# Nine places of raw weights for seven and twelve units for fourteen; the residual leaves SBUF during cross-attention; a weight split moves ahead of a sum

## The chip, the core and the metric

The kernel runs on one core of one Trainium2 chip. The time is device microseconds of one execution; the median of several runs counts. A core has a matmul engine (TensorE, in the profile PE, its weight loads PEld), VectorE (DVE), ScalarE (ACT), GpSimd (POOL) and SyncE (SP). Each engine takes its instructions in a fixed order and waits on semaphores. SyncE issues most DMAs here, GpSimd some. SBUF is the on-chip memory that the engines work in, PSUM holds the matmuls' sums in eight banks.

## The reference

Two layers work on one residual stream `x` of 256 rows by 2048 columns in f32. Each layer has three sub-layers, each behind an RMS norm and added to `x`:

```
x = x + attention(rms_norm(x))          # layer 0: differential attention, layer 1: latent attention
x = x + cross_attention(rms_norm(x), mem_h)   # 256 memory rows, 4 heads of 128
x = x + square(relu(rms_norm(x) @ wup)) @ wdown     # 2048 -> 8192 -> 2048
```

A last RMS norm closes it. All weights are f32, some 410 MB in all.

## The kernel before, in words

**The products.** TensorE works on pairs of rounded parts: every f32 operand is split into a high half (a rounded copy) and a low half (the rest), and a product is three matmuls: high by high, high by low, low by high (`unit_part`, L238 to L249). The activations live split in SBUF in tiles called units (`unit`, 8 KB of each partition). The weights are loaded a block of 512 by 512 at a time (1 MB, 8 KB of each partition) into a raw tile; `halves_of` (L205) splits it in two pieces. For each piece ScalarE writes the high half (`whi`, L201) and VectorE the low half (`wlo`, L202). There are four buffers for each half, so at most four pieces are ahead of TensorE.

**The pools.** `wraw` has `RAWS` = 7 places for raw tiles, `units` has `UNITS` = 14 places for units. Both kinds of places have the same size. A load into a raw tile waits until the tile that had its place before has been read for the last time.

**What sets the order.** TensorE's order is written out by hand: the program keeps a clock of its own and puts small tasks (transposes, attention) between the products (`Task`, `pump`). The DMAs stay in the order in which the program issues them (`load`, L173). The orders of VectorE, ScalarE and GpSimd are chosen when the program is built: a scheduler estimates when each operand is there and takes, of what it thinks is ready, what stands earliest in the source. On the chip each engine then waits at whatever instruction stands next. `fill` (L215) keeps four weight blocks split ahead in the source, and fetches the next block's raw data once more ahead.

**The MLP's up projection.** Its 8192 columns come in eight blocks. Block 0 is done plainly. Blocks 1 to 7 use Strassen's scheme (`Seven`, L819): the 2 by 2 blocks of rows and columns of activations and weights are combined, so that seven products p1 to p7 do the work of eight. Each product has two steps (x = 0, 1), each of one raw tile. The combined activations (`Forms`) are made at the end of cross-attention on VectorE (L454, L471, L443). The combined weights are made in place: `add` (L843) is a VectorE sum of two raw tiles, 2048 elements wide. The tile t is loaded with the 12 block; for p5 the 11 block is added to it, for p6 the 22 block is added to it, for p2 the 21 block; behind p3's split GpSimd issues an accumulating DMA that adds the 12 block into the 22 tile for p7 (L835). So each block has six L843 sums: two for p5, two for p6, two for p2. The results of the products are combined on VectorE (L915, L919, L922). Steps of the down projection of earlier blocks are put between the products by a planner (`mlp_line`).

**The p2 job.** Its function first adds the 21 tile to t (L873), then splits the 21 tile. The sum reads the 21 tile and changes t, the split reads the 21 tile alone; p4 later uses t.

**The residual.** `x` lies in DRAM (`xd`, eight pieces of 128 by 512) for most of the time. Sub-layers that don't need its rows add to it with an accumulating DMA on GpSimd's queue (L504). `fetch_residual` (L506) allocates two units and loads the rows on GpSimd's queue, 8 DMAs of 256 KB; `store_residual` (L513) stores one piece. The last group of an attention (`project_group` with `nxt`, L1172) fetches it, adds its product in SBUF (`add_residual`, L500), and feeds the next norm (squares on ScalarE at L379, transposes on TensorE at L163). The two units then stay in use through cross-attention. `project_out` (L1162) adds cross-attention's product to the same tiles, feeds the forms of the MLP's norm, and stores the pieces. A norm's `row_norm` takes the power of -0.5 on GpSimd (L385), so this stands in GpSimd's order with the DMAs.

Of the kernel before, what the change touches and what calls it, by code (L numbers as in the profile page):

```python
# [21 lines left out]
CH = 512  # L22
EPS = 1e-6
WARM = 9
RAWS = 7
MLP_BLOCKS = 8
SEVEN = (1, 2, 3, 4, 5, 6, 7)
EVS = 7
UNITS = 14

T_EV, T_TURN, T_ROT, T_SM, T_SQ, T_ADD, T_NORM, T_SUM = 2.6, 2.6, 12.0, 6.5, 4.4, 2.2, 7.2, 3.0

# [16 lines left out]
def trunk(ctx, tc, x, xT, xT0, mem, memT, positions, gcols, gfinal, lam_vecs, consts, W, out):  # L49
    nc = tc.nc  # L50

    def pool(name, bufs, space=None):
        kw = {"space": space} if space else {}
        return ctx.enter_context(tc.tile_pool(name=name, bufs=bufs, **kw))

    keep = pool("keep", 1)
    wraw = pool("wraw", RAWS)
    whalf = pool("whalf", 4)
    units = pool("units", UNITS)
    work = pool("work", 2)  # L60
# [10 lines left out]
    def unit():  # L71
        return units.tile([P, 2, 4, S], F32R, tag="unit", name=nm("unit"))
# [92 lines left out]
    def f32(ap):  # L165
        return ap.bitcast(F32)
# [5 lines left out]
    def load(dst, src, queue=None):  # L172
        tc.keep_in_program_order((queue or nc.sync).dma_start(dst, src))  # L173
# [31 lines left out]
    def halves_of(raw, n=4 * CH, pieces=2):  # L205
        split = split_pieces(raw, n, pieces)
        for _ in range(pieces):
            split.next()
        return split.halves
# [41 lines left out]
    def matmul_chunk(acts, width=CH, turns=False, by_k=False):  # L251


        ps = [bank("mm") for _ in range(NT)]
        n = len(acts)

        def part(u, h, hi, lo, t):
            unit_part(ps[t][:, :width], acts[u], h, hi, lo, t, u == 0, u == n - 1)

        def ready_unit(u):  # L260
            need(acts[u].tasks)

        for u in range(n - 2 if turns else n):
            for h, (hi, lo) in enumerate(take()):
                ready_unit(u)
                if by_k and u == 0:
                    for k in range(2):
                        at = slice(k * width, (k + 1) * width)
                        for t in range(NT):
                            ah, al = acts[0].get(0, 2 * h + k, t), acts[0].get(1, 2 * h + k, t)  # L270
                            mm3(ps[t][:, :width], ah, al, hi[:, at], lo[:, at], h + k == 0, False)
                    continue
                for t in range(NT):
                    part(u, h, hi, lo, t)
        if turns:
            parts = [(u, h, *w) for u in (n - 2, n - 1) for h, w in enumerate(take())]
            for u in (n - 2, n - 1):
                ready_unit(u)
            for t in range(NT):
                for p in parts:  # L280
                    part(*p, t)
        return ps
# [214 lines left out]
    def add_residual(t, c, ps, later=False):  # L497
        if not later:
            xc = xs[t][:, c * CH : (c + 1) * CH]
            nc.vector.tensor_tensor(xc, xc, ps, ALU.add)  # L500
            return
        e = work.tile([P, CH], F32, tag="ev", name=nm("add"), bufs=EVS)
        nc.scalar.copy(e, ps)  # L503
        tc.keep_in_program_order(nc.gpsimd.dma_start(xd[t][c], e, accum_op=ALU.add))  # L504

    def fetch_residual():  # L506
        for t in range(NT):
            xs[t] = f32(unit()).rearrange("p a k t -> p (a k t)")
        for c in range(4):
            for t in range(NT):  # L510
                load(xs[t][:, c * CH : (c + 1) * CH], xd[t][c], nc.gpsimd)

    def store_residual(t, c):  # L513
        load(xd[t][c], xs[t][:, c * CH : (c + 1) * CH], nc.gpsimd)
# [304 lines left out]
    class Seven:  # L819
# [21 lines left out]
        def job(self, p, x):  # L841
            def add(o, q):
                nc.vector.tensor_tensor(o, o, q, ALU.add)  # L843

            loads = {"p5": (("t", x), (0, 1)), "p6": ((22, x), (1, 1)), "p2": ((21, x), (1, 0))}

            def fetch():
                key, (i, j) = loads[p]
                if key not in self.raw:
                    self.raw[key] = self.fetch(i, j, x)  # L850

            def run():
                r = self.raw
                if p in loads:
                    fetch()
                if p == "p1":
                    r[11, x] = o = self.fetch(0, 0, x)
                elif p == "p5":
                    o = r["t", x]
                    add(o, r.pop((11, x)))  # L860
                elif p == "p6":
                    o = r["t", x]
                    add(o, r[22, x])
                elif p == "p3":
                    o = r[22, x]
                    split = halves_of(o)
                    self.fetch(0, 1, x, o)
                    return split
                elif p == "p7":
                    o = r.pop((22, x))  # L870
                elif p == "p2":
                    o = r.pop((21, x))
                    add(r["t", x], o)  # L873
                else:
                    o = r.pop(("t", x))
                return halves_of(o)

            if p in loads:
                run.fetch = fetch
            return run  # L880
# [280 lines left out]

    def project_out(acts_o, gcol):  # L1162
        nxt = Forms(gcol)
        for c in range(4):
            ps = matmul_chunk(acts_o)
            for t in range(NT):
                add_residual(t, c, ps[t])
                nxt.feed(c, t, ps[t])
                store_residual(t, c)
        return nxt  # L1170

    def project_group(o, nxt=None, each=None):  # L1172
        if nxt:
            fetch_residual()
        for c in range(4):
            ps = matmul_chunk([o])
            if each:
                each(c)
            for t in range(NT):
                add_residual(t, c, ps[t], not nxt)  # L1180
                if nxt:
                    nxt.feed(c, t, ps[t])

    def attention(project, attend, mid, gcol):


        held = project(0)
        last = None
        m = []
        for gi in range(4):  # L1190
            o = Held(unit())
            attend(held, o)
            if last is not None:
                project_group(last, each=(lambda c: m.append(given_unit(memT, c, G_MEM))) if gi == 3 else None)
            if gi < 3:
                held = project(gi + 1)
            mid(gi)
            last = o
        mk = mem_keys(m)
        nxt = Stream(gcol)  # L1200
        project_group(last, nxt)
        return nxt, m, mk

    def cross(l, norm, m, mk):
        a = norm.done()
        rq = keep2(norm.rstd, SC_CA, "rq")
        q = Held(unit())
        ps = matmul_chunk(a)
        for t in range(NT):
            heads_T(ps[t], t, rq[t], q)  # L1210
        o = Held(unit())
        mv = []
        attend4(
            lambda h, first: whole(q, mk, h, S), q.tasks + mk.tasks,
            lambda: mv[0] if mv else None, o, False,
        )
        mv.append(mem_values(m))
        return project_out([o], G_MLP + 16 * l)
# [360 lines left out]
def build(a, w):  # L1579
    import concourse.bacc as bacc  # L1580

    nc = bacc.Bacc("TRN2", target_bir_lowering=False, num_devices=1, dynamic_dma_scratch_size=1024)
    arrays = {}

    def dram(name, v):
        arrays[f"in_{name}_dram"] = v
        return nc.dram_tensor(f"in_{name}_dram", v.shape, mybir.dt.from_np(v.dtype), kind="ExternalInput").ap()

    args = [dram(k, a[k]) for k in ("x", "xT", "xT0", "mem", "memT", "positions", "gcols", "gfinal", "lam_vecs", "consts")]
    weights = {k: dram(k, v) for k, v in w.items()}  # L1590
    o = nc.dram_tensor("out_0_dram", (S, D), F32, kind="ExternalOutput").ap()
    with tile.TileContext(nc, schedule_with_timeline_sim=True) as tc, tc.manual_schedule(engines={mybir.EngineType.PE}):
        trunk(tc, *args, weights, o)
    return nc, arrays
# [8 lines left out]
```

## Time and profile before

| what | value |
|---|---|
| median of 3 runs | 2225.3 us (2225.22 to 2227.26) |
| the profiled execution | 2232.52 us |
| its span, first to last instruction | 2230.8 us |
| mean granted clock of TensorE | 0.997 |
| HBM read, written | 459.24 MB, 37.75 MB |

How to read the profile: times count from the span's start. In a timeline a row is start, duration, engine, line, operation, output and inputs by the program's names, shapes, number of merged instructions, and in brackets the idle time before it with what ended it. In the waits a row is who waited for whom: total time, how often, the longest. In the busy times by stretch the columns are the length, then busy time (and number) of PE, PEld, DVE, ACT, POOL, then the granted clock of TensorE, the busy share of the DMA engines, and GB/s. The chain is the work that ended last, followed back. A row of DMA issues ends with the median time from issue to landing. Matmuls of 128x512 overlap: a row's duration is longer than its share of time.

Attention and cross-attention of layer 0 fill the first 500 us, its MLP the time to about 1180; layer 1 follows, with its MLP from about 1540 to the end.

### The profile page before, as it was taken

What the parts mean: (1) busy time and instruction counts of PE and PEld (TensorE: products, weight loads), DVE (VectorE), ACT (ScalarE), POOL (GpSimd) and SP (SyncE); (2) the same over time, 40 slices, a digit from 0 to 9 for tenths busy, and PEclk for the clock granted to TensorE, in tenths of its full rate; (3) what the DMA queues carried; (4) which work ended last, traced back from release to release, by engine and by line L of the source; (5) the groups of instructions that cost most, each with busy time, mean ns of one, the idle gap of its engine ahead of it and who ended that gap; (6) DMA issues with size and microseconds to landing.
All of it is one profiled execution on the core that took longest, in us unless ns stands there. A gap on an engine that the chain in (4) does not pass through costs nothing.

```text
span 2230.8 us, 28094 instructions
## 1 busy us (share of the span) xinstructions
PE 2209.2 (99%) x10559; PEld 1847.0 (83%) x10559; DVE 1673.8 (75%) x1801; ACT 1413.6 (63%) x1929; POOL 260.5 (12%) x390
## 2 busy tenths in 40 slices
PE   9999999999999999999999999999999999999998
PEld 7888888888888888887889988888888888888786
DVE  6665657789778788788665877668987887887864
ACT  6555646666766666666655766656766666666664
POOL 1212212000000000000100422201000000000011
PEclk9999999999999999999999999999999999999999
DMA  9457668446967876876955466935778678678691
GB/s 388 190 160 259 198 220 262 181 170 203 288 196 237 256 215 234 261 212 219 293 216 194 138 187 207 304 130 193 260 227 245 208 261 237 209 256 240 195 327 66
DMA packets 89785, 498.83 MB, mean 224 GB/s; under 512 B 10672, under 2 KB 11056, under 8 KB 37680
## 3 DMA queue, kind: packets, MB, share of 16 engines
q1 hardware_dynamic: 65232, 423.09, 51.6%
q0 software_dynamic: 24128, 73.41, 16.9%
q8 instruction: 83, 1.36, 0.2%
q10 hardware_dynamic: 288, 0.52, 0.1%
q14 instruction: 54, 0.44, 0.1%
HBM read 459.24 MB, written 37.75 MB: 223 GB/s over the span
## 4 chain that ended last, share of the span: by engine, by line
PE 81%; DVE 7%; DMA 5%; issue 4%; ACT 2%; POOL 1%; DVEq 0%; ACTq 0%; POOLq 0%
PE mm L159 59%; PE pr L159 17%; DMA raw<-in_mlp_wup_dram 5%; DVE wlo L202 4%; PE ax L159 3%; PE ax L163 2%; ACT whi L201 1%; PE mm L163 1%; DVE raw L843 1%; DVE unit L342 0%; DVE raw L471 0%; DVE unit L443 0%; POOL rs L385 0%; ACT p L1236 0%; ACT p L1237 0%
## 5 line engine op out<-in xcount | busy, mean ns | idle before, releaser
L202 DVE TENSOR_TENSOR wlo<-raw,whi 128x1024 fp32r<-128x1024 f32 (+2 forms) x962 | 1149.6, 1213 | 405.6 <-ACT whi L201 386.4
L201 ACT CAST whi<-raw 128x1024 fp32r<-128x1024 f32 (+2 forms) x962 | 998.4, 1041 | 642.3 <-PE mm L159 535.9
L159 PE MATMUL mm<-whi,unit 128*128 128x512 f32 (+3 forms) x4416 | 1394.4, 388 | 2.1 <-DVE unit L342 1.3
L159 PEld LDWEIGHTS mm<-whi,unit 128*128 128x128 f32 x4416 | 824.9, 188 | 164.4 <-DVE unit L342 2.2
L159 PE MATMUL mm<-wlo,unit 128*128 128x512 f32 (+3 forms) x2208 | 851.2, 386 | 0.8 <-DVE wlo L202 0.8
L159 PE MATMUL pr<-whi,unit 128*128 128x512 f32 x1568 | 508.4, 393 | 6.9 <-DVE p L919 6.9
L159 PEld LDWEIGHTS mm<-wlo,unit 128*128 128x128 f32 x2208 | 415.3, 188 | 79.0 <-DVE wlo L202 2.6
L159 PEld LDWEIGHTS pr<-whi,unit 128*128 128x128 f32 x1568 | 295.9, 189 | 70.7 <-issue 9.7
L159 PE MATMUL pr<-wlo,unit 128*128 128x512 f32 x784 | 307.7, 392 | 1.6 <-DVE wlo L202 0.6
L843 DVE TENSOR_TENSOR raw<-raw,raw 128x2048 f32<-128x2048 f32 x84 | 192.3, 2289 | 66.2 <-DMA raw<-in_mlp_wup_dram 66.2
L159 PEld LDWEIGHTS pr<-wlo,unit 128*128 128x128 f32 x784 | 148.0, 189 | 35.6 <-DVE wlo L202 5.8
L504 POOL DMA_DIRECT2D xd<-add x104 | 91.3, 913 | 616.0 <-ACT add L503 586.6
L835 POOL DMA_DIRECT2D raw<-in_mlp_wup_dram x28 | 24.9, 889 | 714.0 <-DVE wlo L202 673.3
L503 ACT COPY add<-mm 128x512 f32<-128x512 f32 x104 | 59.8, 588 | 9.9 <-PE mm L159 9.1
L1236 ACT ACTIVATE p<-p,r 128x512 f32<-128x512 f32 x42 | 30.4, 723 | 30.1 <-DVE p L919 21.4
L341 ACT CAST unit<-ax 128x512 fp32r<-128x512 f32 x64 | 37.2, 581 | 16.1 <-PE ax L163 16.1
L159 PE MATMUL mm<-unit,whi 128*128 128x256 f32 x256 | 47.1, 285 | 0.1
L163 PE MATMUL ax<-identr,p 128*128 128x128 f32 x304 | 46.1, 272 | 0.0
L163 PEld LDWEIGHTS ax<-identr,p 128*128 128x128 f32 x304 | 37.8, 139 | 9.9
L342 DVE TENSOR_TENSOR unit<-ax,unit 128x512 fp32r<-128x512 f32 x64 | 43.9, 685 | 1.2 <-ACT unit L341 1.0
L385 POOL TENSOR_TENSOR rs<-rs,mhalf 128x1 f32<-128x1 f32 (+1 forms) x28 | 25.2, 903 | 161.0 <-DVE rs L384 161.0
L159 PEld LDWEIGHTS mm<-unit,whi 128*128 128x128 f32 x256 | 40.0, 192 | 0.4 <-DVE unit L342 0.3
(170 smaller groups left out, 1147.2 us busy)
## 6 DMA issues: line engine op xcount, KB each, us to landing
raw<-in_mlp_wup_dram SPq DMA_DIRECT2D x128, 1024.0 KB, 5.8
raw<-in_mlp_wdown_dram SPq DMA_DIRECT2D x128, 1024.0 KB, 5.9
raw<-in_da_wqkv_dram SPq DMA_DIRECT2D x45, 1024.0 KB, 9.0
raw<-in_mlp_wup_dram POOLq DMA_DIRECT2D x28, 1024.0 KB, 7.9
xd<-add POOLq DMA_DIRECT2D x104, 256.0 KB, 6.1
raw<-in_da_wo_dram SPq DMA_DIRECT2D x16, 1024.0 KB, 5.0
raw<-in_ca_wkv_dram SPq DMA_DIRECT2D x16, 1024.0 KB, 5.0
raw<-in_mla_wo_dram SPq DMA_DIRECT2D x16, 1024.0 KB, 9.7
```

The lines of the kernel that those rows point to most:

```text
L159: return nc.tensor.matmul(o, stationary, moving, start=start, stop=stop, skip_group_check=onto)
L163: nc.tensor.transpose(o, src, ident)
L201: nc.scalar.copy(hi, r)
L202: nc.vector.tensor_tensor(lo, r, f32(hi), ALU.subtract)
L341: nc.scalar.copy(hi, src)
L342: nc.vector.tensor_tensor(dst[:, 1, :n, t * P : (t + 1) * P], src, f32(hi), ALU.subtract)
L385: nc.gpsimd.tensor_tensor(r[:, :n], r[:, :n], mhalf.broadcast_to([P, n]), ALU.pow)
L503: nc.scalar.copy(e, ps)
L504: tc.keep_in_program_order(nc.gpsimd.dma_start(xd[t][c], e, accum_op=ALU.add))
L835: tc.keep_in_program_order(nc.gpsimd.dma_start(onto, src, accum_op=ALU.add))
L843: nc.vector.tensor_tensor(o, o, q, ALU.add)
L1236: nc.scalar.activation(r, src, AF.Relu, scale=rstd[t])
```

## The change

Four edits, no other:

- `RAWS` 7 becomes 9 and `UNITS` 14 becomes 12. The SBUF that two units had goes to two raw tiles.
- `project_group` stores each piece of the residual to DRAM as soon as the next norm has been fed from it, when it is the last group of an attention. The two units are free when the stores and the norm have read them.
- `project_out` fetches the residual again ahead of its products into two new units. For each layer this is 8 stores and 8 fetches of 256 KB more, all on GpSimd's queue.
- In the p2 job the split of the 21 tile comes ahead of the sum into t.

```diff
-RAWS = 7
+RAWS = 9
...
-UNITS = 14
+UNITS = 12
...
                 elif p == "p2":
                     o = r.pop((21, x))
+                    split = halves_of(o)
                     add(r["t", x], o)
+                    return split
...
     def project_out(acts_o, gcol):
         nxt = Forms(gcol)
+        fetch_residual()
         for c in range(4):
...
                 if nxt:
                     nxt.feed(c, t, ps[t])
+                    store_residual(t, c)
```

In the built program the orders of TensorE and SyncE are the same as before. GpSimd's has the 32 added DMAs. VectorE's and ScalarE's have the same instructions in another order at some places, most of them L843 sums in the MLPs and the work around the end of cross-attention.

## Prediction

> **What bounds the kernel now.** I read the page first, then busy time by stretch, the waits, the chain, and last the timelines of one block.
>
> ```profile
> span 2230.8 us, 28094 instructions
> PE 2209.2 (99%) x10559; PEld 1847.0 (83%) x10559; DVE 1673.8 (75%) x1801; ACT 1413.6 (63%) x1929; POOL 260.5 (12%) x390
> ```
> ```profile
> 500.00:1100.00 600.00, 596.09 (x2668) 490.33 (x2667) 494.19 (x420) 399.93 (x454) 38.92 (x42) 1.00 0.75 235
> 1540.00:2140.00 600.00, 594.54 (x2658) 488.26 (x2657) 493.49 (x422) 396.18 (x449) 39.16 (x42) 1.00 0.75 232
> ```
> The matmul engine is busy for 2209.2 of 2230.8 us, so no edit that leaves the matmuls alone can gain much; it can lose a lot if something new makes them wait. In the two MLPs (the stretches above; columns PE, PEld, DVE, ACT, POOL) VectorE is busy 494 of 600 us and stands close behind TensorE. What TensorE still loses to others is small:
>
> ```profile
> PE pr L159 <- DVE p L919: 6.9, 6, 2.2
> PE mm L159 <- DVE wlo L202: 0.8, 2, 0.5
> ```
> ```profile
> DVE raw L843 <- DMA raw<-in_mlp_wup_dram: 66.2, 34, 4.3
> ```
> ```profile
> SPq L173 <- DVE wlo L202: 1719.0, 338, 15.4
> ```
> Behind those 7.7 us stands the third row: VectorE's sums of two weight blocks (L843) wait 66.2 us for weights to land. Behind that stands the fourth: the load queue waits for a place that a low half (L202) gives free. One block shows the sequence:
>
> ```profile
> 1006.82 6.73 DMA raw<-in_mlp_wup_dram
> ...
> 1017.13 7.91 DMA raw<-in_mlp_wup_dram
> ...
> 1028.80 5.98 PE pr L159 x18
> 1049.74 4.11 PE mm L159 x18
> ```
> ```profile
> 1029.74:1033.15 3.41, 3.41 (x9) 2.65 (x9) 3.29 (x4) 2.24 (x3) 0.00 (x0) 0.50 0.67 214
> 2074.22:2077.63 3.41, 3.21 (x8) 2.57 (x9) 3.29 (x4) 2.57 (x4) 0.00 (x0) 0.50 0.35 74
> ```
> ```profile
> 1028.80 0.47 PE L159 MATMUL pr<-whi,unit 128*128 128x512 f32 x1 [2.12 <-DVE p L919]
> ```
> A place is free at 1006.82 and 1017.13, the weights land 6.73 and 7.91 us later, the sums run, then L919, and TensorE has waited 2.12 us. Then comes a second price: the granted clock is 0.50 for 3.41 us, and 18 matmuls take 5.98 instead of 4.11 us, 1.9 more. It happens twice in the run (second row).
>
> **The change part by part.**
>
> Nine places. Each load takes the place that a load two further back gave free, so a load is issued when before issued the one two ahead of it. SyncE's order is the same. The second load of p5's first sum, issued at 1006.82 before (chain above), now goes out at 1000.15:
>
> ```profile
> 1000.15 0.33 SPq L173 DMA_DIRECT2D raw<-in_mlp_wdown_dram  x1
> ```
> With sums left where they were, the 66.2 us would go, and with them the 6.9 and 0.8 us and both clock drops (1.9 each): 7.7 + 3.8 = 11.5 us. That is all there is to gain.
>
> But the sums don't stay. In the built program the order of VectorE is another one: in ten of the fourteen Strassen-like blocks (the third to the seventh of each layer) the first sum of p5 stands six to eight places earlier. These are the instructions that it passes, as before ran them:
>
> ```profile
> 1002.82 1.23 DVE L202 TENSOR_TENSOR wlo<-raw,whi 128x1024 fp32r<-128x1024 f32 x1 [0.97 <-ACT whi L201]
> 1004.21 3.94 DVE L202 TENSOR_TENSOR wlo<-raw,whi 128x1024 fp32r<-128x1024 f32 x3 [0.16 <-ACT whi L201]
> 1008.07 0.68 DVE L922 TENSOR_TENSOR p<-pr,p 128x512 f32<-128x512 f32 x1
> 1008.67 1.22 DVE L202 TENSOR_TENSOR wlo<-raw,whi 128x1024 fp32r<-128x1024 f32 x1
> 1011.15 1.23 DVE L202 TENSOR_TENSOR wlo<-raw,whi 128x1024 fp32r<-128x1024 f32 x1 [1.26 <-ACT whi L201]
> 1013.67 2.29 DVE L843 TENSOR_TENSOR raw<-raw,raw 128x2048 f32<-128x2048 f32 x1 [1.30 <-DMA raw<-in_mlp_wup_dram]
> ```
> ```profile
> 1007.23 0.39 PE L159 MATMUL mm<-wlo,unit 128*128 128x512 f32 x1
> ```
> The sum now stands right behind the first row, so VectorE comes to it at 1002.82 + 1.23 = 1004.05. If its load takes 6.73 us as before, it lands at 1000.15 + 6.73 = 1006.88; VectorE stands still for 2.8 us; the sum ends at 1009.17; the low half that began at 1004.21 ends 1.22 us later, at 1010.39. TensorE wants it at 1007.23 (last row): it waits about 3.1 us. In general the wait is the load's duration less 3.6 us. Queued behind the sum are five low halves and L922, so it is the next product and not p5 that is late. VectorE needs 1.22 us for a low half and TensorE 1.36 for the six matmuls of a Strassen product (18 in 4.11), so the lateness is caught up by the following ones and paid once per block. The chain has this load for seven of the ten blocks (first and last shown):
>
> ```profile
> 753.35 6.51 DMA raw<-in_mlp_wup_dram
> ...
> 2052.30 7.72 DMA raw<-in_mlp_wup_dram
> ```
> The mean of the seven, between 5.58 and 7.72, is 6.60, hence 3.0 us a block, **30 us** for ten. The ends: a load as quick as those of the attention output (5.0 us) gives 1.4 us a block, 14 us; the slowest in this stretch (8.2) gives 4.6 a block, 46 us.
>
> ```profile
> raw<-in_da_wo_dram SPq DMA_DIRECT2D x16, 1024.0 KB, 5.0
> ```
> ```profile
> DMA to landing us min/median/max: 5.1/6.9/8.2
> ```
> I take 6.6, since the loads keep their order and their neighbours. In the first two blocks of a layer the places are free earlier, and low halves are ready well ahead: nothing.
>
> The clock: waits of 2.1 us cost 1.9 more. Of the seven loads five make a wait over 2.1 us, so seven of ten drops, 7 x 1.9 = **13 us**. Ends: none, and all ten (19).
>
> The Trainium skill, "TensorE: Matmul & The Clock Gate", section "What's actually happening", has the clock halve only after an idle window of about 3.4 us, against the 2.12 us of this trace; by its rule the waits of this forecast would mostly go without that price. The trace decides: the drop follows a wait of 2.12 us.
>
> The split ahead of its sum (p2). Both take the same data, so nothing is added. The first p2 sum of a block keeps its place, the second goes nine places forward, between the two low halves of the last row here:
>
> ```profile
> 987.29 0.33 SPq L173 DMA_DIRECT2D raw<-in_mlp_wup_dram  x1
> ```
> ```profile
> 970.28 0.33 SPq L173 DMA_DIRECT2D raw<-in_mlp_wdown_dram  x1
> ```
> ```profile
> 994.42 2.29 DVE L843 TENSOR_TENSOR raw<-raw,raw 128x2048 f32<-128x2048 f32 x1 [2.93 <-DMA raw<-in_mlp_wup_dram]
> ```
> ```profile
> 976.52 2.59 DVE L202 TENSOR_TENSOR wlo<-raw,whi 128x1024 fp32r<-128x1024 f32 x2
> ```
> Its load, issued at 987.29 and there at 994.4 (7.1 us), now goes out at 970.28 and is there at 977.4; VectorE comes to the sum at 977.7. I cost it at nothing; were the load 2 us later, about 1 us a block would be late, 10 us.
>
> The entry to each MLP: p5's first sum now passes two residual sums.
>
> ```profile
> 492.57 0.68 DVE L500 TENSOR_TENSOR unit<-unit,mm 128x512 f32<-128x512 f32 x1
> ...
> 493.77 0.68 DVE L500 TENSOR_TENSOR unit<-unit,mm 128x512 f32<-128x512 f32 x1
> ...
> 495.50 2.29 DVE L843 TENSOR_TENSOR raw<-raw,raw 128x2048 f32<-128x2048 f32 x1
> ```
> ```profile
> 495.33 0.27 PE L163 MATMUL mm<-identr,unit 128*128 128x128 f32 x1
> ```
> The second L500 ends 2.29 later, at 496.7; its four transposes would start about 0.4 us after 495.33: 1 us of waiting, **2 us** for two layers (0 to 4).
>
> Residual out of SBUF during cross-attention: 16 stores and 16 fetches more, all on GpSimd's queue.
>
> ```profile
> 418.64 2.12 POOL L385 TENSOR_TENSOR rs<-rs,mhalf 128x1 f32<-128x1 f32 x2 [37.54 <-DVE rs L384]
> ```
> ```profile
> 439.82 1.04 PE L163 MATMUL mm<-identr,ev 128*128 128x128 f32 x8
> ```
> ```profile
> 473.28 1.28 DVE L500 TENSOR_TENSOR unit<-unit,mm 128x512 f32<-128x512 f32 x2
> ```
> ```profile
> unit<-xd POOLq DMA_DIRECT2D x32, 256.0 KB, 11.9
> ```
> The stores stand ahead of the two L385, which may start a microsecond later; what they scale is turned over by TensorE only at 439.82, some 20 us on. The fetches follow at 421, when the last transposes of the old copy are over, take about 8 x 0.6 us to issue and 12 to land, 440 at the latest, and the sums that read them come at 473: 33 us of cover. Nothing, at most 2 us a layer.
>
> Twelve units: counted from first write to last read in the records of before, eleven are in use at most, and in the changed order every unit's place is free over 25 us before its next write. Nothing.
>
> **Sum**: 30 + 13 + 2 - 11.5 = +33.5 us. It is made on the profiled execution (2232.5 us, span 2230.8), which is 0.3% over the median of 2225.3; the terms are waits, so I add them to the median: **2259 us**.
>
> **The rivals.**
>
> *Loads in time (faster).* If a load issued 6.7 us earlier is there when VectorE comes (under 3.6 us, the point where the wait vanishes), only the gain remains: 2225.3 - 11.5 + 2 = 2216. For it: two places more is what the 66.2 us ask for. Against: the shortest load above takes 5.0.
>
> *Loads at 5.0 us.* 14 + 2 - 11.5: 2230, no drop of the clock. For it: deeper prefetch spreads the loads. Against: where the load now starts, the DMA engines were full before (share 0.99 in this row):
>
> ```profile
> 1000.00:1004.00 4.00, 4.00 (x20) 3.33 (x19) 3.03 (x4) 2.52 (x3) 0.00 (x0) 1.00 0.99 287
> ```
>
> *Loads at 8.2 us.* 46 + 19 + 2 - 11.5 = +55.5: 2281. For it: the engines' share in that row. Against: only one load of that stretch took so long.
>
> *No drop of the clock.* The drop comes twice in before, each time after a wait of over 2 us, but it may need a longer one or a chance alignment: without it 33.5 - 13 gives 2246. By the rule of the Trainium skill's page named above this would be the time.
>
> *The change doesn't do what it says*: loads bound by something else than places, order of no consequence: 2225. Against: the fourth row of the waits, 1719 us of the queue waiting for L202.
>
> **How the numbers follow.** Forecast 2259 (2.4 to 3.6 us per block with the drops): 0.45. Loads at 8.2: 0.15. No drop: 0.15. Loads at 5.0: 0.12 (half within 0.2%, half above). Loads in time: 0.08. No effect: 0.05. A measurement of this kernel can tell 0.2%, 4.5 us, from no change. So faster 0.08, same 0.05 + 0.06 = 0.11, slower 0.81. The range leaves out the loads in time and what of the slowest case lies above its own estimate: 2223 to 2281.
>
> **What would show it.** In the changed profile: the idle time ahead of L843 is still there (some 40 us), ten times 2 to 4 us, now followed by low halves; TensorE waits for "DVE wlo L202" some 30 us in about ten places instead of 0.8, no more for L919; the granted clock falls to 0.50 behind several of them; cross-attention unchanged. It is wrong if the L843 rows wait for nothing, or if TensorE's waits for L202 stay under 5 us in total.

## The result, and the profile after

| | before | after |
|---|---|---|
| median, same chip | 2226.74 us (2225.22 to 2228.06, 6 runs) | 2240.65 us (2233.67 to 2247.49, 6 runs) |
| ratio, 95% interval | | 1.0061 (1.0041 to 1.0080) |
| profiled execution | 2232.52 us, span 2230.8 | 2233.67 us, span 2231.8 |

The change makes the kernel slower, as forecast, but by 14 us and not by 34: the forecast of 2259 us is 18 us too high. The two profiled executions are hardly apart, since before's is slower than before's median and after's is the fastest of its six. So the traces show the mechanism, and the medians what it costs on average.

The page of after, first its span and busy times, then the two MLPs (columns PE, PEld, DVE, ACT, POOL, granted clock, DMA share, GB/s):

```profile
span 2231.8 us, 28183 instructions
PE 2206.2 (99%) x10559; PEld 1844.6 (83%) x10559; DVE 1673.0 (75%) x1801; ACT 1413.9 (63%) x1929; POOL 278.9 (12%) x422
```
```profile
500.00:1100.00 600.00, 595.71 (x2672) 490.06 (x2671) 495.13 (x422) 400.26 (x453) 39.54 (x43) 1.00 0.75 236
1540.00:2140.00 600.00, 592.99 (x2659) 487.18 (x2658) 493.11 (x422) 397.18 (x453) 40.16 (x43) 1.00 0.74 233
```

The engines are as busy as before. The waits of after (total us, times, longest) have changed places:

```profile
DVE raw L843 <- DMA raw<-in_mlp_wup_dram: 33.6, 23, 3.1
PE mm L159 <- DVE wlo L202: 10.3, 8, 2.6
PE mm L163 <- DVE unit L500: 1.1, 2, 0.5
```

There is no wait of TensorE for a piece of p1 any more (L919 before, 6.9 us), VectorE's waits for weights are half of what they were, and TensorE waits eight times for a low half: 10.3 us where it was 0.8. The timeline of VectorE in after, in the block that the prediction worked through:

```profile
999.70 1.22 DVE L202 TENSOR_TENSOR wlo<-raw,whi 128x1024 fp32r<-128x1024 f32 x1 [1.49 <-ACT whi L201]
1002.42 1.22 DVE L202 TENSOR_TENSOR wlo<-raw,whi 128x1024 fp32r<-128x1024 f32 x1 [1.50 <-ACT whi L201]
1003.75 0.69 DVE L342 TENSOR_TENSOR unit<-ax,unit 128x512 fp32r<-128x512 f32 x1
1005.61 1.22 DVE L202 TENSOR_TENSOR wlo<-raw,whi 128x1024 fp32r<-128x1024 f32 x1 [1.16 <-ACT whi L201]
1007.34 2.29 DVE L843 TENSOR_TENSOR raw<-raw,raw 128x2048 f32<-128x2048 f32 x1 [0.51 <-DMA raw<-in_mlp_wup_dram]
1009.54 3.49 DVE L202 TENSOR_TENSOR wlo<-raw,whi 128x1024 fp32r<-128x1024 f32 x3
```

The sum (L843) stands where the prediction had it, with its low halves queued behind. It waits 0.51 us for its load, not 2.8. To compare times of two kernels they are told against the same matmul of TensorE, just ahead of the place where it waits. These rows are of before, after, and after again (the wait):

```profile
1007.00 0.39 PE L159 MATMUL mm<-whi,unit 128*128 128x512 f32 x1
```
```profile
1009.79 0.39 PE L159 MATMUL mm<-whi,unit 128*128 128x512 f32 x1
1010.82 0.50 PE L159 MATMUL mm<-wlo,unit 128*128 128x512 f32 x1 [0.64 <-DVE wlo L202]
```

After runs 2.79 us behind before's times here. The step between two such matmuls is 0.23 us in before (1007.00 to 1007.23) and 1.03 at the wait: TensorE loses 0.80 us in this block.

### The profile page after: what moved, and what is told of

It reads as the page before. It is cut to its first block, busy times and chain, and to the rows that moved or that the text cites. A ratio compares the mean times of both kernels' runs of the same rounds, so it can differ in the third digit from the quotient of the medians.

```text
span 2231.8 us, 28183 instructions
## 1 busy us (share of the span) xinstructions
PE 2206.2 (99%) x10559; PEld 1844.6 (83%) x10559; DVE 1673.0 (75%) x1801; ACT 1413.9 (63%) x1929; POOL 278.9 (12%) x422
## 4 chain that ended last, share of the span: by engine, by line
PE 88%; DVE 4%; DMA 3%; issue 2%; ACT 2%; POOL 0%; DVEq 0%; ACTq 0%; POOLq 0%
PE mm L159 65%; PE pr L159 18%; DMA raw<-in_mlp_wup_dram 3%; PE ax L159 3%; DVE wlo L202 2%; PE ax L163 2%; ACT whi L201 1%; PE mm L163 1%; DVE raw L843 1%; ACT p L1240 0%; ACT p L1241 0%; DMA raw<-in_da_wqkv_dram 0%; DVE unit L342 0%; DVE unit L500 0%; DVE unit L443 0%
## 5 line engine op out<-in xcount | busy, mean ns | idle before, releaser
L159 PE MATMUL mm<-wlo,unit 128*128 128x512 f32 (+3 forms) x2208 | 851.9, 386 | 10.3 <-DVE wlo L202 10.3
L843 DVE TENSOR_TENSOR raw<-raw,raw 128x2048 f32<-128x2048 f32 x84 | 192.0, 2285 | 33.7 <-DMA raw<-in_mlp_wup_dram 33.6
L173 POOL DMA_DIRECT2D xd<-unit x40 | 21.8, 544 | 255.4 <-DVE unit L500 255.0
```

What stands on the lines that cost most here:

```text
L159: return nc.tensor.matmul(o, stationary, moving, start=start, stop=stop, skip_group_check=onto)
```

## Experiments

Times are medians; each ratio is against the kernel before, run on the same chip in the same series, with its 95% interval. In the first series the kernel before took 2229.39 us (23 runs), in the second 2228.67 (22 runs), in the third 2229.37 (29 runs). The ratios are those on record; the ratio of two medians can differ from them by 0.1%. Theory 1 is that the loss comes from p5's first sum, which VectorE meets before its load has landed, and that the other three edits are free; the rivals are named in each expectation.

### The three other edits: free

**The change without the split ahead of p2's sum** (order of all engines as in the change):

```diff
                     o = r.pop((21, x))
-                    split = halves_of(o)
                     add(r["t", x], o)
-                    return split
```

> The change with the p2 job as before (sum ahead of its split). Theory 1 (what costs is the order of VectorE that came with nine places, not the p2 edit): the built order of every engine is the same as in the change, so the time is the change's, 1.003 to 1.010 of before, and the profile is a second look at the change: L843 idle for some 30 us, TensorE waiting for L202 8 to 12 us in about eight to ten places. Rival (the p2 edit matters, through something that the order doesn't show): a time near before's, 0.998 to 1.002. If the runs scatter by 10 us again, time should fall with the mean granted clock, about 2 to 3 us for 0.001.

Measured: 2239.05 us, ratio 1.0044 (1.0028 to 1.0060), the change's own time within its scatter. The waits of its profile:

```profile
PE mm L159 <- DVE wlo L202: 15.0, 8, 3.6
```

The same eight waits, longer this time, since the eight loads took longer: 5.97 to 9.18 us, against 6.26 to 8.21 in the change. In the two traces every engine has the same instructions in the same order, and the intervals overlap, so the line edit has no effect that these runs can tell.

**The residual out of SBUF alone**, seven places and fourteen units:

```diff
         nxt = Forms(gcol)
+        fetch_residual()
...
                     nxt.feed(c, t, ps[t])
+                    store_residual(t, c)
```

> Before with the residual out of SBUF during cross-attention as the only edit (7 places, 14 units). Theory 1: 32 more DMAs on GpSimd's queue are hidden, 0.999 to 1.001 of before, L843 idle 66 us as before. Rival 2 (the change's loss is the added traffic and GpSimd's queue): 1.004 to 1.008, with waits in cross-attention (373 to 500 us of the span) that before doesn't have.

Measured: 2231.53 us, ratio 1.0001 (0.9986 to 1.0016). Free.

**The change with seven places**: twelve units, residual out, split ahead.

```diff
-RAWS = 9
+RAWS = 7
```

> The change with seven places of raw weights, as before: twelve units, the residual out of SBUF, the split ahead of the sum. The order of VectorE's sums is that of the kernel before. Theory (these three are free, the two places are the whole change): 2225 to 2232 us, ratio within 0.2% of 1, waits on L919 of some us again. Rival (two units fewer hold back what writes them): over 2235 us, with waits for a unit.

Measured: 2230.69 us, ratio 1.0007 (0.9994 to 1.0020). So the loss comes with the two places, and the other edits together are free. On VectorE and ScalarE the trace has the order of the kernel before. The old waits are back, under the line that L919 has here:

```profile
PE pr L159 <- DVE p L921: 7.2, 8, 2.5
```

### Where the sum stands

**The sums kept in program order**, first in the change, then in the kernel before. They then stand right ahead of their own halves; in the fourth to the seventh Strassen block of a layer p5's first sum comes 11 low halves later than before.

```diff
-                nc.vector.tensor_tensor(o, o, q, ALU.add)
+                tc.keep_in_program_order(nc.vector.tensor_tensor(o, o, q, ALU.add))
```

> The change, with each L843 sum pinned behind the VectorE instruction that the source has ahead of it; the sums then stand five to twelve low halves later than in before instead of up to eight earlier. Theory 1: loads are there when VectorE comes, L843 idle under 3 us in total, TensorE's waits for L202 under 2 us, none for L919, no drop of the clock: 0.994 to 0.997 of before, that is 2214 to 2220 us. Rival 3 (a sum of 2.29 us right ahead of its own low halves makes these late, so the wait only changes its place): TensorE waits for L202 over 10 us, 1.000 or above.

> Before (7 places, 14 units, residual kept) with each L843 sum pinned in the same way. Theory 1: what matters is the place of the sum against its load, not the number of places; the loads land 15 us ahead of the pinned sums even with seven places: 0.994 to 0.997 of before, L843 idle under 10 us. Rival 4 (nine places are needed for it): L843 still idle over 30 us and 0.999 or above.

Measured: 2290.6 us, ratio 1.0265 (1.0237 to 1.0294), and 2274.09 us, ratio 1.0190 (1.0164 to 1.0216). A sum can be too late as well as too early, which theory 1 had left out. The waits of the change with its sums kept in order:

```profile
PE pr L159 <- DVE wlo L202: 22.1, 20, 1.8
PE pr L159 <- ACT whi L201: 12.8, 8, 1.6
```

VectorE doesn't wait for weights at L843 here, but TensorE waits for high and low halves, 34.9 us in these two rows, and the granted clock falls to 0.50 eight times, for 3.4 or 6.8 us. In the kernel before with its sums kept in order the second p2 sums still wait, 35.9 us in all, so theory 1 was missed there on both counts, the waits and the time. The prediction had no price for a late sum. Which of the sums does it was left to the next two runs.

**p5's sum alone made late**, by writing it over the block of p1 in place of t: it must then wait until p1's own halves are made, and comes 8 to 11 low halves later than before in all but the first Strassen block of a layer.

```diff
-                    o = r["t", x]
-                    add(o, r.pop((11, x)))
+                    q, o = r["t", x], r.pop((11, x))
+                    add(o, q)
+                    r["t", x] = o
```

> The change, but p5's sum is written over the other block of weights (its first product's own), so it can only run after that product's low halves were made; in the built order p5's two sums stand 8 to 10 low halves later than in the kernel before, 13 to 15 later than in the change, and the p2 sums stay where the change has them. Theory 1 (what made the pinned kernels slow is a p5 sum close ahead of its own high and low halves, which ScalarE and VectorE make one after the other): no wait of VectorE for p5's loads, two waits of TensorE in each of ten blocks, of about 1.75 us for a high half and 2.0 us for a low half, 38 us, and some drops of the clock: 2265 to 2285 us. Rival (the pinned kernels were slow by the p6 and p2 sums, and p5's late place is harmless): neither the waits of the change nor new ones, 2215 to 2222 us.

Measured: 2257.44 us, ratio 1.0130 (1.0116 to 1.0144). The kind of loss was right, its size was not:

```profile
PE pr L159 <- DVE wlo L202: 32.2, 20, 1.7
```

Twenty waits, as expected, but all for low halves, two in each of eight blocks and one in each of four, and no drop of the clock, for which the expectation had added some. 32 us of waits stand against 28.8 by the medians. p5's sum, then, costs at both ends. p6's sums were not tried alone.

**p2's sum made late, nine places**, by writing it over p2's own block, behind that block's split:

```diff
                     split = halves_of(o)
-                    add(r["t", x], o)
+                    add(o, r["t", x])
+                    r["t", x] = o
                     return split
```

> The change, but p2's sum is written over p2's own block of weights after that block was split, so it stands behind p2's own low halves: 12 and 6 low halves later than in the kernel before, where the change had 0 and 8 earlier. With it p5's sums come 3 low halves earlier than in the kernel before, not 5 and 4. Theory 1 (TensorE's waits in the change come from p5's first sum meeting a load that is 0.5 to 3.1 us late; 2 low halves are 2.4 us of VectorE, and p2's late sums are far enough ahead of p4): p5's waits shrink to under 0.5 us a block, the waits on L919 stay away, 2215 to 2225 us. Rival (a late p2 sum is what the pinned kernels paid for, about 2 us a block in fourteen blocks): 2250 to 2260 us.

Measured: 2224.88 us, ratio 0.9985 (0.9976 to 0.9994): with nine places still, the loss is gone. A late p2 sum is harmless; the likely reason is that p4, which needs it, comes much later. In the eight blocks VectorE now reaches p5's first sum, which stands 2 low halves later than in the change, after its load is there. What is left of the waits:

```profile
DVE raw L843 <- DMA raw<-in_mlp_wup_dram: 9.7, 8, 2.5
PE pr L159 <- DVE wlo L202: 3.4, 4, 1.6
```

They are nearly all in the second and third block of a layer. With the same nine places the loss comes and goes with the place of the sums.

### Why the wait was 1.2 us and not 3

**Seven places, residual out, p2's sum turned.** The prediction took a load to go out when before sent the one two ahead of it. If that one was itself held up by something that the change moves, the rule is wrong. In before the second p2 sum waits 2.93 us and runs 2.29 (the row at 994.42 in the prediction), ahead of the low halves that give the places free.

> The kernel with the residual out of SBUF, but seven places and fourteen units as before, and p2's sum turned over p2's own block behind its split: p2's sums stand 12 and 6 low halves later than in the kernel before, p5's stay (0 or 1 later). Theory 1 (in the kernel before, the second p2 sum waits 2.9 us for its load and runs 2.3 us ahead of the low halves that free the places of p5's loads): without that wait the places come free some 2 us or more earlier, p5's loads land before their sums, the waits of TensorE on L919 go and with them the drops of the clock: 2215 to 2222 us. Rival A (the places are freed no sooner): as before, 2226 to 2231 us. Rival B (a late p2 sum costs about 2 us a block): 2250 to 2260 us.

Measured: 2221.82 us, ratio 0.9972 (0.9961 to 0.9983), faster than both kernels. The load that before issued at 1000.15 is this one here, and the matmul at 1007.00 is the second row:

```profile
998.07 0.33 SPq L173 DMA_DIRECT2D raw<-in_mlp_wdown_dram  x1
```
```profile
1006.91 0.39 PE L159 MATMUL mm<-whi,unit 128*128 128x512 f32 x1
```

This kernel is 0.09 us ahead of before here, so the load goes out 1000.15 - (998.07 + 0.09) = 2.0 us sooner, with the same number of places. Of VectorE's sums only p2's have moved by more than 2 low halves. In the change, p5's load takes just this turn:

```profile
1000.95 0.33 SPq L173 DMA_DIRECT2D raw<-in_mlp_wup_dram  x1
```

Less the 2.79 us it is 998.16 on before's clock: 2.0 us before the forecast's 1000.15. The expectation was not right in all: p5's first sum still waits for its load here, only the second doesn't. VectorE in this kernel:

```profile
1016.52 2.29 DVE L843 TENSOR_TENSOR raw<-raw,raw 128x2048 f32<-128x2048 f32 x1 [1.66 <-DMA raw<-in_mlp_wup_dram]
1018.73 3.49 DVE L202 TENSOR_TENSOR wlo<-raw,whi 128x1024 fp32r<-128x1024 f32 x3
1022.13 0.68 DVE L342 TENSOR_TENSOR unit<-ax,unit 128x512 fp32r<-128x512 f32 x1
1022.73 0.68 DVE L922 TENSOR_TENSOR p<-p,pr 128x512 f32<-128x512 f32 x1
1023.33 1.22 DVE L202 TENSOR_TENSOR wlo<-raw,whi 128x1024 fp32r<-128x1024 f32 x1
1024.46 2.28 DVE L843 TENSOR_TENSOR raw<-raw,raw 128x2048 f32<-128x2048 f32 x1
```

L922 is the piece of p1 for which TensorE waited in before (L919 there). It stands ahead of the second sum now, and so isn't held up by it. The wait at the first sum is covered.

**Only p2's sum turned**, nothing else: the kernel before with the last diff, the split ahead included.

> The kernel before with nothing but p2's sum turned over its own block, behind its split: seven places, fourteen units, the residual in SBUF. Theory (what stands in VectorE's way in the kernel before is the second p2 sum with its wait of 2.9 us): the gain of the run with the residual out of SBUF comes without it: 2219 to 2224 us, a ratio of 0.996 to 0.998. Rival (the residual's place out of SBUF had a part in it): 2226 to 2231 us.

Measured: 2222.38 us, ratio 0.9969 (0.9960 to 0.9978). The gain needs neither places nor the residual's move.

### The dose

**Eight places and thirteen units**, first as in the change, then with p2's sum turned:

```diff
-RAWS = 9
+RAWS = 8
...
-UNITS = 12
+UNITS = 13
```

> The change with eight places of raw weights and thirteen units: p5's sums stand 1 and 3 low halves earlier than in the kernel before (5 and 4 in the change), the second p2 sum 4 earlier (8 in the change). Theory 1 (the loss is a load that lands after VectorE has come to a sum that was moved too far): the sum stands about 4 low halves, 5 us, later than in the change and its load is issued one place, 2 to 3 us, later: hardly a wait for it, and the waits on L919 are at least halved; 2218 to 2227 us. Rival (the loss goes with the number of places, whatever the order): half of the change's loss, 2232 to 2236 us.

> Eight places of raw weights, thirteen units, residual out of SBUF, and p2's sum turned over its own block behind its split. p5's first sums stand where the kernel before has them or 2 low halves earlier. Theory (one place more brings the load of p5's first sum one release of a place forward, and the sum hardly moves): TensorE doesn't wait for p5, as with seven places; 2219 to 2224 us, no clear difference from the seven places. Rival (every further place moves the sum more than the load): 2225 to 2232 us.

Measured: 2229.48 us, ratio 0.9999 (0.9990 to 1.0009), and 2223.18 us, ratio 0.9978 (0.9968 to 0.9988). With eight places in the change's order no wait of TensorE is left in the blocks of the change's eight; two are in the third block of a layer, where p5's first sum comes 4 low halves earlier than before, and each is followed by a drop of the clock. The waits on L919 are gone, and these took their place:

```profile
PE mm L159 <- DVE wlo L202: 6.1, 2, 3.5
PE mm L163 <- DVE unit L500: 1.6, 2, 0.8
```

So 2218 to 2227 was missed by 2.5 us, and so was the rival's 2232 to 2236: the loss doesn't go with the number of places, but theory 1 had left out a block with an order of its own. With p2's sum turned, eight places give nothing over seven.

## Why the prediction was right or wrong

**Right: where the loss would be.** p5's first sum stands earlier than its load, and the low halves behind it are late for the next product, as named. Eight blocks show it, not ten: in the third block of a layer VectorE waits as well, 1.17 us in layer 0 (the row below) and 3.13 us in layer 1, but TensorE doesn't. Why these two are spared is left open.

```profile
662.62 2.29 DVE L843 TENSOR_TENSOR raw<-raw,raw 128x2048 f32<-128x2048 f32 x1 [1.17 <-DMA raw<-in_mlp_wup_dram]
```

**Wrong: the rule "a load is issued when before issued the one two ahead of it"**, and with it the 3.0 us a block. That issue, at 1000.15, was late in before because a low half stood behind p2's second sum with its wait. The change takes that sum out of the way, eight low halves forward, and the place comes free 2.0 us sooner; the run with seven places shows the same 2.0 us without the nine places. So it is in all eight blocks: told against the same matmul, the change sends this load 1.14 to 2.54 us before the forecast's time, 1.90 us in the mean, and in the run with seven places the place comes free sooner by the same time in each block, to 0.01 us. The prediction had seen the sum move, and had checked only whether its own load would be in time. It had told of the move under the split; but VectorE's order is the same without the split's move, and it is that of the kernel before with the split and seven places, so the move came with the nine places. The load's duration was not the error. The chain of after has all eight:

```profile
745.01 6.53 DMA raw<-in_mlp_wup_dram
830.17 6.57 DMA raw<-in_mlp_wup_dram
915.35 6.97 DMA raw<-in_mlp_wup_dram
1000.95 6.26 DMA raw<-in_mlp_wup_dram
```
```profile
1788.97 8.21 DMA raw<-in_mlp_wup_dram
1875.79 7.02 DMA raw<-in_mlp_wup_dram
1961.42 6.77 DMA raw<-in_mlp_wup_dram
2046.84 6.90 DMA raw<-in_mlp_wup_dram
```

Their mean is 6.90 us (6.60 forecast). TensorE's losses, measured like the 0.80 us above, are 1.07, 1.11, 1.52, 0.80, 2.75, 1.56, 1.31 and 1.44 us. Each is its load's duration less 5.46 us, to 0.01 us or so. In the run of the same order without the split's move the loads took other times, and the eight losses, 0.51 to 3.72 us, are again the durations less 5.46. The rule's form held, its 3.6 was 1.9 too small. The sum is 11.6 us, where 30 stood.

**Wrong in size: seven drops of the clock, 13 us.** Shorter waits, fewer drops. The profiled execution has none, the profile of the change without the split's move (15.0 us of waits) has three. And a wait over 2.1 us isn't enough for a drop; see the last section. Over after's six runs the mean granted clock falls from 0.999 to 0.995 as the time grows from 2233.67 to 2247.49. A drop of 3.41 us at 0.50 takes 0.5 x 3.41 / 2232 = 0.0008 off that mean, so the slowest run has room for some five drops. These runs have no trace, so the number of drops in them is an estimate.

**Right: the entry to the MLP** (2 us forecast; 0.71 us each, 1.4 us, measured start to start), the residual, the split and the units at nothing, and the L919 waits and both drops gone.

**Wrong: the start of the sum.** With these sizes the sum on the profiled execution is 11.6 + 1.4 - 11.5 = +1.5 us; 1.15 was measured. But the prediction put its sum onto the median. The profiled execution of before was 7.2 us over the median of 2225.3, and held two drops and 7.7 us of waits, which are the 11.5 us it set against the loss. Another profile of the same MLP order, that of the residual alone, has these waits and no drop:

```profile
PE pr L159 <- DVE p L919: 2.7, 4, 1.5
PE mm L159 <- DVE wlo L202: 0.4, 1, 0.4
```

There the gain to be had is 3.1 us, and this run took 2224.53 us. The profile of the change with seven places, the same order again, has 7.2 us of waits, one drop and 2231.20 us. Of the 74 runs of before in the three series, 42 had a mean granted clock of 0.999 and only 5 had 0.997 or less, as the profiled one had. So a typical run of before has less to lose than 11.5. On the other side, the profile of the change without the split's move lost 16.3 us in its eight blocks and had three drops, at 2244.87 us; and of the 18 runs of that order only after's profiled one had 0.999, the others 0.995 to 0.998. So a typical run of after has more to pay than 11.6. That this is why the medians are 14 us apart and the profiles 1 is inferred from these neighbours, since no run near the median of either kernel has a trace. This error worked against the other two, and hid part of them.

**The rivals.** "Loads at 5.0 us" would have needed quicker loads; none of the eight was under 6.26, and yet its 14 us for the blocks nearly came out, by earlier issue. "No drop of the clock" was right for the profiled execution alone.

## What to carry to other kernels

More buffers move more than the load that they are meant for: a list scheduler puts what reads the load forward as well, and a consumer that sits in an in-order queue can come too early as easily as too late. When the time of a trace is used as a bound for a moved load, ask what set that time; here it was a sum that the same change moved out of the way. To take a sum out of the way, choose which operand it overwrites: written over its own block it stood where its result was wanted late, and 7 us were gained without a buffer.

## What the runs showed of the hardware

The granted clock is decided on a fixed grid. Where a trace has several drops, they begin whole multiples of 3.413 us apart: 1044.48 us in before (2074.22 - 1029.74) are 306 of them. In the change without the split's move three drops begin at 1016.84, 1808.73 and 2068.15, 232 and 76 steps apart. That gives the grid, and the waits can be laid on it. Two waits of TensorE in that run:

```profile
758.80 0.50 PE L159 MATMUL mm<-wlo,unit 128*128 128x512 f32 x1 [3.28 <-DVE wlo L202]
```
```profile
2066.76 0.50 PE L159 MATMUL mm<-wlo,unit 128*128 128x512 f32 x1 [1.94 <-DVE wlo L202]
```

and the cells of the grid around them (first the two that the first wait fell in, then the one with the second wait and the one after it):

```profile
754.01:757.43 3.42, 1.51 (x7) 0.93 (x5) 2.11 (x1) 2.06 (x2) 0.00 (x0) 1.00 0.67 274
757.43:760.84 3.41, 2.04 (x9) 1.70 (x10) 3.41 (x4) 0.00 (x0) 0.00 (x0) 1.00 0.02 5
...
2064.74:2068.15 3.41, 1.47 (x7) 1.18 (x7) 3.41 (x4) 0.93 (x1) 0.00 (x0) 1.00 0.31 127
2068.15:2071.57 3.42, 3.42 (x10) 2.65 (x9) 2.55 (x3) 0.87 (x1) 0.00 (x0) 0.50 0.79 263
```

The wait of 3.28 us is split over two cells and costs nothing more; the wait of 1.94 us falls into one cell with other short gaps, and the next cell runs at 0.50. Counted so over all thirteen traces, from the gaps between starts of matmuls beyond their usual step, each of the drops between a run's start and its end (20 in six traces) follows a cell with at least 2.15 us of gaps, and the fullest cell at full clock that no drop follows has 2.14; the count is good to some 0.02 us. In the run with p5's sum turned no cell has more than 1.98 us, and its twenty waits, of 1.5 to 1.7 us, made no drop at all. The Trainium skill, "TensorE: Matmul & The Clock Gate", section "What's actually happening", has a free-running window of 3413 ns, and the traces agree; that it takes an idle window to halve the clock they don't bear out, since 2.15 us of 3.41 were enough. For a prediction this means a chance and not a threshold: a wait of 2.2 us drops the clock only if it falls into one cell nearly whole, and the phase differs from run to run: the change has no drop in its trace, and the run of the same order without the split's move has three.
